# Down projection of an encoder layer: operands of products 5 and 6 split half by half, two stores on GpSimd's queue

## The chip, the cores and the metric

The kernel runs on one core of a Trainium2 chip. A core has a matrix engine (TensorE, in the profile PE, with its weight loads as PEld), a vector engine (VectorE, DVE), an engine for activation functions and scaled copies (ScalarE, ACT), a general engine (GpSimd, POOL) and an engine that here issues transfers (SyncE, SP). Each engine takes its instructions in a fixed order; semaphores make it wait for others. Transfers (DMA) are issued by an engine's queue and run beside the engines. On-chip memory is SBUF, with 128 partitions; matmuls accumulate in eight banks of PSUM.

The metric is the device time of one execution in microseconds (us): the median of the runs.

## The reference, cut to what matters

One hybrid encoder layer on 1024 positions of width 1024: a norm and an input projection, two groups of attention heads, an output projection and residual, then a gated MLP with a short convolution. The change lies at the end of the MLP, in the product with `w_down`:

```
def conv_ffn(h, w_up, conv_w, conv_b, w_down):
    u = h @ w_up
    u = lax.conv_general_dilated(u, conv_w[:, None, :], ..., feature_group_count=c) + conv_b
    gate, val = u[..., :D_FF], u[..., D_FF:]
    return (jax.nn.gelu(gate) * val) @ w_down

...
x = x + conv_ffn(rms_norm(x, norm2_g), w_up, conv_w, conv_b, w_down)
```

D_FF is 2816, so the last product is (1024 x 2816) by (2816 x 1024), in float32.

## The kernel before

**Seven products for eight.** Both MLP products are done as two-by-two blocks with seven block products in place of eight (a scheme with shared sums, its products numbered 1 to 7). The down projection runs them in the order 1, 5, 6, 3, 7, 2, 4. So product 1 comes first, and products 5 and 6 are the second and third. The contraction of 2816 is cut into 11 pairs of 128-row blocks, q = 0 to 10. One step is one product for one q: 7 x 11 = 77 steps, in the list `steps` (L1427), numbered m = 0 to 76 here. Steps 0 to 10 are product 1, steps 11 to 21 product 5, steps 22 to 32 product 6, steps 33 to 43 product 3, then 7, 2 and 4.

**float32 from two parts.** An operand is rounded to the matmul type (fp32r) by a copy on ACT, and what the rounding lost is taken by a subtraction on DVE. Three matmuls (high x high, high x low, low x high) then make one product. In `down` (L1474) a step makes 4 row tiles of 3 matmuls, 12 in all, each 128 x 128 by 128 x 512.

**What a step needs.** A block of `w_down` (128 x 512), a block of the gated activations from the scratch tensor `gscr` in DRAM (128 x 512, the stationary side of the matmuls), and for products 5 and 7 a second block of `w_down`, to be subtracted. The activations' sums and differences for the seven products were made earlier, on POOL, and stored to `gscr`; each product has its columns there (`place`, L1391).

**Loads.** `d_load` (L1432) issues two transfers of 256 KB, L1437 for `w_down` and L1438 for `gscr`, side by side into one of four load buffers `F_DR[m % 4]`. `d_load2` (L1440) issues the third, L1443, into one of three buffers `F_D2[q % 3]`. All are on SP's queue.

**Preparation.** `d_prep` (L1445) makes, where the product wants it, a difference on DVE (L1450): for product 5 into `F_T[q]`, which product 6 overwrites with its own and product 4 reads at the end. Then it splits both blocks in one go: the copy on ACT (L1460) and the subtraction on DVE (L1461), 1024 columns each, into one of six operand buffers `R_D[m % 6]`. For products 5 and 6 the first half of the source is `F_T[q]` and the second half lies in the load buffer, at `o + 512`; the two are given as one access pattern whose outer stride is the distance of the two places (L1459).

**Where things lie.** All of this is in two big arrays of SBUF, `bigf` (float32) and `bigr` (fp32r), at fixed columns. The columns of `bigf` that matter: `F_T[0..7]` at 4928 + 512 i; `F_T[8..10]` at 9024 + 512 i; `F_D2` at 3904, 4416 and 11072; `F_DR` at 14656, 15680, 16704 and 11584, 1024 columns each; the residual rows `C_11` at 12608 + 512 t, which are the same columns as two accumulators of the last pair of activations (called s1 and s3 in `gate_sums`).

**Order.** The program is written out step by step (L1594): matmuls of step m, preparation of step m + 3, subtrahend of step m + 6, loads of step m + 7, and what follows a product (`behind`, L1486): sums of finished banks with result rows on DVE (L1470), fetches of residual rows from `rscr` (L1467) in steps q = 5 to 8 of products 1, 5, 6 and 2, and result stores. A compiler pass derives the waits from which columns an instruction reads and writes, and fixes the order on each engine by its own estimate of when things are ready; so a queue's order is close to the program's, but not the same.

**The last pair of activations.** Its convolution, gate and sums come after the down projection has begun: `take(gate_sums(last), 4)` at m = 3 (L1604). `gate_sums` (L1393) stores the gated blocks (L1404, L1405), makes four sums of 128 x 512 on POOL (L1396, with two one-element instructions, L1401, that only order them) and stores two results of 1024 columns each, s1 at L1415 and s3 at L1419. All these stores are on SP's queue, ahead of the loads that follow in the program.

Of the kernel before, what the change touches and what calls it, by code (L numbers as in the profile page):

```python
# [14 lines left out]
AF = mybir.ActivationFunctionType  # L15
OP = mybir.AluOpType
# [7 lines left out]
NPAIR = NBLK  # L24
# [102 lines left out]
def tile_encoder_layer(ctx, tc, x, w_in, gains, outg, norm1_g, norm2_g, w_out, w_up, conv_w, conv_b,  # L127
# [14 lines left out]
    def emit(bounded):  # L142

        act = nc.scalar.activation
        vec = nc.vector
        gp = nc.gpsimd
        mm = nc.tensor.matmul
        dma = nc.sync.dma_start

        def f(off, n):  # L150
            return bigf[:, off:off + n]

        def r(off, n):
            return bigr[:, off:off + n]

        def rf(off, n):
            return bigr[:, off:off + n].bitcast(F32)

        def raw_ap(base, dims):
            return bass.AP(tensor=base.tensor, offset=base.offset,  # L160
                           ap=[list(base.ap[0])] + [list(d) for d in dims])

        def fp(off, *dims):
            return raw_ap(bigf[:, off:off + 1], dims)

        def rp(off, *dims):
            return raw_ap(bigr[:, off:off + 1], dims)

        def rfp(off, *dims):
            return raw_ap(bigr[:, off:off + 1].bitcast(F32), dims)  # L170
# [924 lines left out]
        for m in range(len(prods)):  # L1095
            c, n = prods[m]
# [159 lines left out]
        for gs in range(64 + lag + 1):  # L1256
# [15 lines left out]
            h1, s1 = divmod(gs - lag, 8)  # L1272
# [8 lines left out]
            h1, s1 = divmod(gs - lag - 1, 8)  # L1281
# [90 lines left out]
        def acc(j, u):  # L1372
            return F_ACC[(2 * j + u) % 6]
# [19 lines left out]
        def gate_sums(j):  # L1393
            e, o = acc(j, 0), acc(j, 1)
            s1, s3 = acc(j - 1, 0), acc(j - 1, 1)
            t = lambda d, a, b, op: gp.tensor_tensor(f(d, 512), f(a, 512), f(b, 512), op=op)  # L1396
            g = gscr[j // 2]

            def behind_sum(o):

                gp.tensor_tensor(f(o, 1), f(F_S[1], 1), f(F_S[1], 1), op=OP.add)  # L1401

            def halves():
                dma(g[:, 0:512], f(e, 512))  # L1404
                dma(g[:, 512:1536], f(o, 1024))  # L1405
                behind_sum(s1)
                t(s1, e + 512, o + 512, OP.add)

            def third():
                behind_sum(s3)  # L1410
                t(s3, e, e + 512, OP.subtract)

            def second():
                t(s1 + 512, s1, e, OP.subtract)
                dma(g[:, 1536:2560], f(s1, 1024))  # L1415

            def fourth():
                t(s3 + 512, o, s1 + 512, OP.subtract)
                dma(g[:, 2560:3584], f(s3, 1024))  # L1419

            return [halves, second, third, fourth]

# [22 lines left out]
        def d_prep(m):  # L1445
            if m >= len(steps):
                return
            n, q = steps[m]
            o, d, t = F_DR[m % 4], R_D[m % 6], F_T[q]
            sub = lambda out, i0, i1: vec.tensor_tensor(f(out, 512), f(i0, 512), f(i1, 512), op=OP.subtract)  # L1450
            if n == 5:
                sub(t, o, F_D2[q % 3])
            elif n == 6:
                sub(t, o, t)
            elif n == 7:
                sub(o, o, F_D2[q % 3])
            elif n == 4:
                sub(o, o, t)
            src = fp(t, [o + 512 - t, 2], [1, 512]) if n in (5, 6) else fp(o, [512, 2], [1, 512])  # L1459
            act(rp(d, [512, 2], [1, 512]), src, AF.Copy)  # L1460
            vec.tensor_tensor(rp(d + 1024, [512, 2], [1, 512]), src, rfp(d, [512, 2], [1, 512]), op=OP.subtract)  # L1461

        def o_rows(tt, hf):
            return perm_rows(out, tt, D)[:, 512 * hf:512 * hf + 512]
# [102 lines left out]
        for m in range(2, len(order)):  # L1567
            j, n = order[m]
            product(m)
            wu_prep(m + 4)  # L1570

            if n in (2, 4) or n == 3 and j % 2 == 0 or n == 1 and j % 2:
                take(dealt, 1)
            if n == 3 and j < NPAIR - 1:
                conv(j, 0)
                conv(j, 1)
                if j % 2:
                    gate(j, 0)
                    gate(j, 1)
                    dealt += gate_sums(j)  # L1580
            if j == NPAIR - 1:
                if n == 5:
                    for q in range(4):
                        d_load(q)
                if n == 4:
                    d_prep(0)
                    d_load(4)
                if n == 3:
                    d_prep(1)
                    d_prep(2)  # L1590
                    d_load(5)
                    d_load(6)
        last = NPAIR - 1
        for m in range(len(steps)):  # L1594
            n, q = steps[m]
            down(m)
            d_prep(m + 3)
            if m < 2:
                conv(last, m)
            if m == 2:  # L1600
                gate(last, 0)
                gate(last, 1)
            if m == 3:
                take(gate_sums(last), 4)  # L1604
            d_load2(m + 6)
            d_load(m + 7)
            behind(n, q)
# [68 lines left out]
```

## Time and profile before

| | us |
|---|---|
| median of 3 runs | 1301.46 |
| lowest, highest | 1300.12, 1302.01 |
| the profiled execution | 1300.51 |
| its span in the profile | 1298.7 |
| PE busy in the span | 1236.4 |
| DVE busy | 908.5 |
| ACT busy | 637.4 |
| POOL busy | 391.8 |
| first matmul of the down projection | 1047.74 |
| last matmul's end | 1286.76 |

The profile shows one execution. Times in its rows count from the span's start. A group row gives line, engine, operation, shapes and count, then the busy time in all and the mean of one instruction in ns, then the engine's idle time just before these instructions and what ended it. "bigf<-gscr" is a transfer from `gscr` into `bigf`. The rows "DMA to landing" give the time from the issue of a transfer to its completion. In a timeline row, what stands in brackets is the idle time before the instruction and what released it; x4 means that four were merged into one row.

### The profile page before, as it was taken

The page shows a single profiled execution, that of the slowest core. Times are in us where ns is not written, and L with a number is a line of the kernel's source. Part 1 is how long each engine was busy: PE and PEld are TensorE (multiplying, and loading weights), DVE is VectorE, ACT ScalarE, POOL GpSimd, SP SyncE. Part 2 cuts the span into 40 slices and gives each one's busy share as a digit, 9 for nine tenths or more (in the row PEclk, how much of TensorE's full clock was granted, in tenths as well). Part 3 has the DMA queues.
Part 4 walks back from the last instruction along what each step waited for, and adds up shares of the span by engine and source line. Part 5 has one row for each costly group of instructions (what it writes and reads, how often), then busy time and mean ns, then how long its engine had stood idle before and what let it go on. Part 6 is the DMA issues. An engine that isn't in the chain of part 4 may idle for free.

```text
span 1298.7 us, 18774 instructions
## 1 busy us (share of the span) xinstructions
PE 1236.4 (95%) x7063; PEld 1061.5 (82%) x7063; DVE 908.5 (70%) x1270; ACT 637.4 (49%) x1001; POOL 391.8 (30%) x300
## 2 busy tenths in 40 slices
PE   7999999999998889999999999999999998889996
PEld 7999998999997777888788888888888886657885
DVE  5988685124107779656999999999999964657672
ACT  7856554566556566535544453444443442234430
POOL 1610143000212230011465675665675530000000
PEclk9999999999999899999999999999999998999998
DMA  7126303000014444413222223232223357448970
GB/s 264 54 84 156 88 5 75 24 17 17 9 25 100 106 107 115 156 65 106 74 105 91 92 93 122 94 117 90 91 96 122 122 183 282 166 148 277 315 242 36
DMA packets 120935, 147.12 MB, mean 113 GB/s; under 512 B 51009, under 2 KB 79489, under 8 KB 120321
## 3 DMA queue, kind: packets, MB, share of 16 engines
q1 hardware_dynamic: 119617, 141.10, 33.6%
q0 software_dynamic: 1216, 4.72, 1.7%
q8 instruction: 57, 0.93, 0.3%
q14 instruction: 45, 0.37, 0.1%
HBM read 107.25 MB, written 33.82 MB: 109 GB/s over the span
## 4 chain that ended last, share of the span: by engine, by line
PE 55%; DVE 18%; issue 4%; DMA 4%; ACT 3%; POOL 1%; SPq 0%; ACTq 0%; DVEq 0%; POOLq 0%
PE ps L696 8%; PE ps L1349 6%; PE ps L1351 6%; PE ps L1350 6%; DVE bigf L1382 6%; PE ps L1481 4%; PE ps L1482 4%; PE ps L1480 4%; PE ps L701 3%; PE ps L702 2%; DVE bigf L1353 2%; PE ps L1004 2%; PE ps L1006 2%; PE ps L1005 2%; DVE bigr L1333 2%
## 5 line engine op out<-in xcount | busy, mean ns | idle before, releaser
L1349 PE MATMUL ps<-bigr 128*128 128x512 f32 x616 | 241.0, 391 | 6.5 <-DVE bigf L1353 5.9
L1350 PE MATMUL ps<-bigr 128*128 128x512 f32 x616 | 239.7, 389 | 0.0
L1351 PE MATMUL ps<-bigr 128*128 128x512 f32 x616 | 239.7, 389 | 0.0
L1382 DVE SCALAR_TENSOR_TENSOR bigf<-bigf 128x768 f32<-128x768 f32 (+1 forms) x176 | 178.8, 1074 | 26.5 <-ACT bigf L1380 26.4
L1332 ACT ACTIVATE bigr<-bigf 128x512 fp32r<-128x512 f32 x154 | 93.2, 625 | 139.3 <-POOL bigf L1324 70.4
L1460 ACT ACTIVATE bigr<-bigf 128x1024 fp32r<-128x1024 f32 x77 | 80.5, 1058 | 148.9 <-DMA bigf<-gscr 57.1
L1349 PEld LDWEIGHTS ps<-bigr 128*128 128x128 f32 x616 | 115.6, 188 | 35.1 <-DVE bigf L1353 9.3
L696 PEld LDWEIGHTS ps<-bigf 128*128 128x128 f32 x1024 | 131.9, 191 | 9.3 <-issue 0.3
L1351 PEld LDWEIGHTS ps<-bigr 128*128 128x128 f32 x616 | 115.6, 188 | 24.2
L1350 PEld LDWEIGHTS ps<-bigr 128*128 128x128 f32 x616 | 115.7, 188 | 23.5
L1461 DVE TENSOR_TENSOR bigr<-bigf,bigr 128x1024 fp32r<-128x1024 f32 x77 | 93.2, 1222 | 57.0 <-ACT bigr L1460 46.8
L1480 PE MATMUL ps<-bigr 128*128 128x512 f32 x308 | 114.1, 401 | 16.6 <-ACT bigr L1460 16.4
L696 PE MATMUL ps<-bigf 128*128 128x65 f32 x1024 | 129.1, 269 | 0.0
L421 PE MATMUL ps<-bigr 128*128 128x256 f32 x448 | 127.3, 284 | 1.2 <-ACT bigf L300 1.2
L1333 DVE TENSOR_TENSOR bigr<-bigf,bigr 128x512 fp32r<-128x512 f32 x112 | 125.3, 1136 | 3.2 <-ACT bigr L1332 2.5
L422 PE MATMUL ps<-bigr 128*128 128x256 f32 x448 | 126.9, 283 | 0.1
L423 PE MATMUL ps<-bigr 128*128 128x256 f32 x448 | 126.7, 283 | 0.0
L1481 PE MATMUL ps<-bigr 128*128 128x512 f32 x308 | 122.6, 400 | 1.4 <-DVE bigr L1461 0.9
L1482 PE MATMUL ps<-bigr 128*128 128x512 f32 x308 | 121.3, 395 | 0.0
L704 ACT ACTIVATE bigf<-ps 128x512 f32<-128x512 f32 x128 | 76.1, 597 | 78.9 <-PE ps L702 77.9
L421 PEld LDWEIGHTS ps<-bigr 128*128 128x128 f32 x448 | 85.8, 192 | 1.8 <-ACT bigf L300 1.6
L422 PEld LDWEIGHTS ps<-bigr 128*128 128x128 f32 x448 | 85.9, 192 | 0.3 <-DVE bigr L405 0.3
(215 smaller groups left out, 2441.8 us busy)
## 6 DMA issues: line engine op xcount, KB each, us to landing
bigf<-w_down SPq DMA_DIRECT2D x99, 256.0 KB, 3.7
bigf<-w_up SPq DMA_DIRECT2D x44, 512.0 KB, 3.6
bigf<-gscr SPq DMA_DIRECT2D x77, 256.0 KB, 3.7
gscr<-bigf SPq DMA_DIRECT2D x33, 512.0 KB, 2.6
bigf<-w_in SPq DMA_DIRECT2D x8, 1024.0 KB, 5.5
bigf<-x SPq DMA_DIRECT2D x15, 512.0 KB, 7.1
bigf<-w_out SPq DMA_DIRECT2D x8, 512.0 KB, 3.6
bigr<-bigr POOLq DMA_DIRECT2D x8, 512.0 KB, 4.7
```

Source lines behind the costliest of these rows:

```text
L421: mm(o, ah, wh, start=(k == 0 and t % 2 == 0 and n != 2), stop=False, skip_group_check=True)
L422: mm(o, ah, wl, start=False, stop=False, skip_group_check=True)
L423: mm(o, al, wh, start=False, stop=(k == 3), skip_group_check=True)
L696: mm(bank(ob, 65, 66 * i), f(slots[kt] + 128 * i, 128), f(F_VA + 132 * kt + 66 * kv, 65), start=(kt == 0 and i == 0), stop=(kt == 7), skip ...
L1333: (gp if n in (2, 4) and m > 3 else vec).tensor_tensor(rp(o + 512, [128, 4], [1, 128]), src, rfp(o, [128, 4], [1, 128]), op=OP.subtract)
L1349: mm(bank(b), wh, th, start=(k == 0 and n in (1, 5, 6, 7)), stop=False, skip_group_check=True)
L1350: mm(bank(b), wh, tl, start=False, stop=False, skip_group_check=True)
L1351: mm(bank(b), wl, th, start=False, stop=(k == 3), skip_group_check=True)
L1382: vec.scalar_tensor_tensor(f(a + o, n), f(i + d, n), w_, f(a + o, n), op0=OP.mult, op1=OP.add)
L1480: mm(o, ah, r(d, 512), start=(q == 0 and n in (1, 5, 2)), stop=False, skip_group_check=True)
L1481: mm(o, ah, r(d + 1024, 512), start=False, stop=False, skip_group_check=True)
L1482: mm(o, al, r(d, 512), start=False, stop=(q == NQ - 1), skip_group_check=True)
```

## The change

In `d_prep`, products 5 and 6 now split their two source blocks one after the other: two ACT copies and two DVE subtractions of 512 columns, each with a plain pattern, in place of one each of 1024 columns with the strided pattern. The other products keep one copy and one subtraction of 1024 columns, written without the two-level pattern; the columns are the same. In `gate_sums` the two stores of s1 and s3 of the last pair are issued by POOL's queue and no longer by SP's; for the other ten pairs nothing changes. Lines after L1397 move down by one.

```
@@ gate_sums @@
             g = gscr[j // 2]
+            put = gp.dma_start if j == NPAIR - 1 else dma
...
             def second():
                 t(s1 + 512, s1, e, OP.subtract)
-                dma(g[:, 1536:2560], f(s1, 1024))
+                put(g[:, 1536:2560], f(s1, 1024))
...
             def fourth():
                 t(s3 + 512, o, s1 + 512, OP.subtract)
-                dma(g[:, 2560:3584], f(s3, 1024))
+                put(g[:, 2560:3584], f(s3, 1024))
@@ d_prep @@
-            src = fp(t, [o + 512 - t, 2], [1, 512]) if n in (5, 6) else fp(o, [512, 2], [1, 512])
-            act(rp(d, [512, 2], [1, 512]), src, AF.Copy)
-            vec.tensor_tensor(rp(d + 1024, [512, 2], [1, 512]), src, rfp(d, [512, 2], [1, 512]), op=OP.subtract)
+            for i, src, w in ((0, t, 512), (512, o + 512, 512)) if n in (5, 6) else ((0, o, 1024),):
+                act(r(d + i, w), f(src, w), AF.Copy)
+                vec.tensor_tensor(r(d + 1024 + i, w), f(src, w), rf(d + i, w), op=OP.subtract)
```

## The prediction

> **What bounds the kernel now.** I read the page first, then stretches of the last stage, then the chain of waits there. The page gives the span of the profiled execution, a TensorE (PE) that is nearly always busy, and the slices in which it is not.
>
> ```profile
> span 1298.7 us, 18774 instructions
> ...
> PE   7999999999998889999999999999999998889996
> ...
> PEclk9999999999999899999999999999999998999998
> ```
>
> Slices of 32.5 us: the 34th to 36th digit of PE (1071 to 1169 us) are 8, and the granted clock dips in the first of them. That is in the down projection. Its 77 steps issue 12 matmuls each, 924 in all. I cut the stage at the start of its first matmul, after step 11, after step 37, and at its last matmul.
>
> ```profile
> core 0: us, PE busy (x) PEld busy (x) DVE busy (x) ACT busy (x) POOL busy (x), PEclk, DMA share, GB/s
> 1047.74:1080.38 32.64, 32.64 (x145) 26.84 (x143) 17.64 (x20) 8.50 (x8) 10.77 (x6) 1.00 0.65 228
> 1080.38:1180.67 100.29, 82.28 (x313) 59.91 (x313) 56.42 (x62) 31.46 (x31) 0.00 (x0) 0.93 0.58 194
> 1180.67:1286.77 106.10, 106.10 (x469) 87.65 (x467) 65.21 (x72) 36.66 (x35) 0.00 (x0) 1.00 0.67 226
> ```
>
> (x) counts matmuls that touch the stretch, so one at a border counts twice. The last stretch holds 39 steps, 468 matmuls in 106.10 us: 0.2267 us each, 2.72 us a step, with PE never idle. The first holds 12 steps at the same pace (32.64 / 12 = 2.72). The middle one holds steps 12 to 37, 312 matmuls, worth 312 x 0.2267 = 70.7 us at that pace; it took 100.29. So **29.6 us are lost there and nowhere else in the stage**: 18.0 us with PE idle (100.29 - 82.28), the rest as slow matmuls while the clock was at 0.93 or an operand was late. Steps 11 to 32 are products 5 and 6, the ones whose source pattern changes; steps 33 to 37, already plain, start with no lead and pay for the last of it.
>
> What does PE wait for? The first stall is that of step 12; then the chain of waits, in order of time:
>
> ```profile
> 1085.47 0.80 PE L1480 MATMUL ps<-bigr 128*128 128x512 f32 x1 [4.93 <-ACT bigr L1460]
> 1084.37 1.06 ACT L1460 ACTIVATE bigr<-bigf 128x1024 fp32r<-128x1024 f32 x1 [9.84 <-DMA bigf<-w_down]
> 1085.46 1.24 DVE bigr L1461
> ...
> 1086.71 0.33 SPq L1437
> ...
> 1087.09 2.93 DMA bigf<-gscr
> ...
> 1090.12 1.07 ACT bigr L1460
> ```
>
> The vector engine (DVE) ends a split (L1461) at 1086.70, the queue issues a load at 1086.71, its second half lands at 1090.02, and only then does the next copy on ScalarE (ACT, L1460) start. Which step is each? Steps load and copy in order, so a count up to that moment tells.
>
> ```profile
> L1438 SPq DMA_DIRECT2D bigf<-gscr x17: 327/424/740, 1003.9 to 1087.1; - x17
> L1460 ACT ACTIVATE bigr<-bigf x14: 1041/1059/1067, 1038.8 to 1090.1; 128x1024 fp32r<-128x1024 f32 x14
> ```
>
> The load of 1087.09 is the 17th, of step 16; the copy of 1090.12 is the 14th, of step 13. **The copy of step 13 waits for the data of step 16, which it does not use.** The pattern explains it: for products 5 and 6 the source is two pieces, t = F_T[q] and o + 512, written as one pattern with stride o + 512 - t. For step 13 (q = 2, buffer 1) the pieces lie at columns 5952 and 16192 of bigf; between them lies load buffer 0 (14656 to 15680), which step 16 fills. A dependence taken from the first to the last column of a pattern sees a conflict where none is. It binds both ways: the load of m + 4 waits for preparation m (truly: same buffer), preparation m + 1 waits for that load (falsely). A link is 0.4 us of queue, 2.9 of transfer, 1.07 of ACT and 1.24 of DVE, 5.7 us, against 2.72 us of matmuls. The spans include the earlier load buffer for buffers 0, 1 and 2, not for 3, so some three steps in four are bound; a late step is also fed in small pieces, as its L1481 waits for DVE.
>
> **Part 1, the split pattern (L1459 to L1461).** It removes the reach of the pattern, so step m waits for its own pieces only. It adds, in 22 steps, one ACT and one DVE instruction. The rows nearest to the new forms, and the old ones:
>
> ```profile
> L1460 ACT ACTIVATE bigr<-bigf 128x1024 fp32r<-128x1024 f32 x77 | 80.5, 1058 | 148.9 <-DMA bigf<-gscr 57.1
> L1332 ACT ACTIVATE bigr<-bigf 128x512 fp32r<-128x512 f32 x48 | 29.0, 625 | 46.7 <-POOL bigf L1324 27.1 <-PE ps L1350 19.3
> L1461 DVE TENSOR_TENSOR bigr<-bigf,bigr 128x1024 fp32r<-128x1024 f32 x77 | 93.2, 1222 | 57.0 <-ACT bigr L1460 46.8
> 1037.70 0.67 DVE L1333 TENSOR_TENSOR bigr<-bigf,bigr 128x512 fp32r<-128x512 f32 x1
> L1450 DVE TENSOR_TENSOR bigf<-bigf 128x512 f32<-128x512 f32 x44 | 29.9, 689 | 29.4 <-DMA bigf<-w_down 29.0
> ```
>
> ACT: 2 x 0.625 - 1.058 = +0.19 us a step; DVE: 2 x 0.67 - 1.22 = +0.12. That is 4.2 and 2.6 us of work in all, but the worst step needs 1.25 us of ACT and 0.69 + 1.34 + 0.69 = 2.7 us of DVE (difference, two halves, one sum into the result, the last in eight of the steps), under or at 2.72, so it hides behind the matmuls as long as preparation is ahead; if not, it costs 0.3 us for each step that PE waits for. The other five products keep the same 1024 columns, written plainly: nothing.
>
> Can loads keep up? Product 7 has the traffic of product 5 and is already plain:
>
> ```profile
> 1197.00:1226.90 29.90, 29.90 (x133) 24.77 (x132) 20.78 (x23) 11.58 (x11) 0.00 (x0) 1.00 0.91 317
> 1070.00:1080.00 10.00, 10.00 (x46) 8.29 (x45) 3.75 (x4) 2.12 (x2) 0.00 (x0) 1.00 0.98 343
> ```
>
> Its 11 steps ran at 2.72 us with three loads each (and four result stores). At 343 GB/s a 256 KB load takes 0.76 us: three make 2.3 us a step, four (the steps that also fetch rows of the residual) 3.06, 0.34 too much in four steps, 1.4 us that the lead covers. So in the steady state PE sets the pace. What is left is the entry, around step 12.
>
> **Part 2, the two stores on the queue of GpSimd (POOL), L1416 and L1420 after the change.** SyncE's queue (SP) now stands still behind them, since their sums are late:
>
> ```profile
> 1057.12 0.32 SPq L1405 DMA_DIRECT2D gscr<-bigf  x1
> 1064.47 0.32 SPq L1415 DMA_DIRECT2D gscr<-bigf  x1
> 1066.97 0.32 SPq L1419 DMA_DIRECT2D gscr<-bigf  x1
> 1067.39 0.38 SPq L1437 DMA_DIRECT2D bigf<-w_down  x1
> ...
> 1070.90 0.43 SPq L1467 DMA_DIRECT2D bigf<-rscr  x1
> 1071.43 0.38 SPq L1443 DMA_DIRECT2D bigf<-w_down  x1
> 1056.09 5.60 POOL L1401 TENSOR_TENSOR bigf<-bigf 128x1 f32<-128x1 f32 x1 [22.18 <-issue]
> 1063.15 3.79 POOL L1396 TENSOR_TENSOR bigf<-bigf 128x512 f32<-128x512 f32 x3
> 1057.01 4.62 DVE L1461 TENSOR_TENSOR bigr<-bigf,bigr 128x1024 fp32r<-128x1024 f32 x4
> ```
>
> From 1057.44 to 1067.39 it issues no load. Moved, the loads of steps 10, 11 and 12 go out when their buffers come free, with the DVE splits that end at 1058.2, 59.4 and 60.5: some 9 us earlier. But the residual rows of L1467 land where s1 lies, so they may not start until the store out of s1 has landed; on SP they, and all behind them, wait for POOL. Its price, from the rows of DMAs:
>
> ```profile
> 394.35 0.56 POOL L788 DMA_DIRECT2D bigr<-bigr  x1 [10.04 <-PE ps L892]
> bigr<-bigr POOLq DMA_DIRECT2D x8, 512.0 KB, 4.7
> gscr<-bigf SPq DMA_DIRECT2D x33, 512.0 KB, 2.6
> DMA to landing us min/median/max: 2.5/5.2/7.7
> ```
>
> From POOL a 512 KB transfer took 4.7 us, four small ones (last row, L344) 2.5 to 7.7; from SP 2.6. The second half of s1 is summed at 1064.4; 4.7 us later is 1069.1 (bounds 1066.9 and 1072.1), against 1070.90 for the rows now. So behind them part 2 gains 1.8 us, or loses 1.2, or gains 4.0. I take 1.8, by the transfer of the same size. POOL itself has nothing after these stores.
>
> **The entry, step by step.** PE is due at step 12 at 1080.38, and 2.72 us later at each one after. Step 12's last input is its subtrahend, now issued at 1071.43; with 1.8 us off and the 5.5 us its landing took, 1075.1; then 0.69 + 1.25 + 0.67 = 2.6 us: ready at 1077.7, in time. Loads for steps 13 to 15 follow at 0.76 us each (two or three a step, plus a row of the residual): ready by some 1080, 1083 and 1086 against 1083.1, 85.8 and 88.5. Step 16 loads into the buffer that step 12 leaves at 1077.7, behind four more residual rows (3.0 us) and 5.5 us of landing: 1086.2, subtrahend a little later, ready near 1090 against 1091.3. From there 2.3 us of loads meet 2.72 us of matmuls, and the lead grows. I leave 1 us for a step that just misses.
>
> ```profile
> DMA to landing us min/median/max: 5.5/5.5/5.5
> ```
>
> **Sum.** The profiled execution took 1300.51 us, 1.8 us around its span; 1300.51 - 29.6 + 1 = 1271.9. The median of the runs shown is 1301.46, 0.95 above: **1272.9 us**.
>
> **Rivals.** *A new wait behind POOL.* DVE and POOL get in each other's way: the L1401 row above, one element, took 5.60 us while DVE ran without a pause to 1061.63. With loads earlier, DVE splits steps 10 and 11 (1.2 + 2.0 us) just when POOL sums: POOL may be 3.2 us later, and the transfer 3.0 longer (7.7 for 4.7). The subtrahend of step 12 then lands at 1075.1 + 6.2 = 1081.3, and step 12 is ready at 1083.9, 3.5 us late; with a second step half as late 5. That is 1272 + 5 = 1277. [...]
>
> *Only part of the stall goes.* The compiler's order on each queue is fixed anew; a queue that waits in a worse order, or subtrahend buffers that come round every third step, could leave a third to a half of 29.6: 1282 to 1287. Against it: product 7, with the same buffers, shows no stall.
>
> *The waits are others' and stay* (the change doesn't do what it says). If the copy of step 13 still starts on the landing of step 16's load, the link of 5.7 us stays and grows by the added 0.19 + 0.12 us; three in four of 22 steps, 16 links, make 5 us: 1306.5, slower. It decides as soon as these links outlast 2.72 us, which they do at any length. Against it: from step 37 on, plain patterns with the same buffers never stall. A variant keeps the waits but hides the additions: 1301.
>
> **How the numbers follow.** Forecast 0.62, the wait behind POOL 0.19, part of the stall 0.10, slower 0.06, no change 0.03. Faster 0.91, the same 0.03 (within 0.2%, about what this kernel's measurement can tell from no change), slower 0.06. More than 29.6 us cannot come from this stall; with 1 us of scatter and no residue the low end is 1270. The high end takes in the rival behind POOL and the better half of the partial one: 1283. That holds 0.62 + 0.19 + 0.05, about 0.8 with some room for scatter.
>
> **What would show it.** Right: the stretch after step 11 at 46 matmuls in 10 us with the clock at 1.00, L1460 no longer idle behind a gscr load, 44 more instructions (22 on ACT, 22 on DVE), halves of 0.6 and 0.67 us; SP loading between 1057 and 1067. Wrong: a copy that starts on the landing of a load three steps on (the waits stay); L1467 late and PE idle near step 12 (POOL); a time above 1283.

## The result, and the profile after

| | before | after |
|---|---|---|
| median, us | 1300.79 (4 runs, 1299.90 to 1302.01) | 1268.59 (4 runs, 1267.77 to 1269.75) |
| ratio | | 0.9748, 95% interval 0.9734 to 0.9763 |
| the profiled execution, us | 1300.51 | 1268.52 |
| its span, us | 1298.7 | 1266.7 |
| first to last matmul of the down projection, us | 239.01 | 209.44 |
| end of the last matmul (its start plus 0.23 us, the pace of the stage) to end of span, us | 11.95 | 9.54 |

The kernel is 32.2 us faster. The forecast was 1272.9 with a range from 1270 to 1283; the result lies 4.3 us below the forecast and 1.4 us below the range. In the profiled executions, the first matmul of the stage starts at 1047.74 before and at 1047.75 after, so all of the gain comes later: 29.57 us inside the stage, 2.41 us behind its last matmul.

The page of after: the span, the busy time of each engine, and the 40 slices (now of 31.7 us).

```profile
span 1266.7 us, 18849 instructions
...
PE 1224.8 (97%) x7063; PEld 1060.7 (84%) x7063; DVE 911.0 (72%) x1292; ACT 640.8 (51%) x1023; POOL 393.8 (31%) x302
...
PE   7999999999999889999999999999999999999997
...
PEclk9999999999999999999999999999999999999999
```

The hole in PE's slices 34 to 36 is closed, and so is the dip of the granted clock there (0.93 over steps 12 to 37 before, 1.00 now). The count of instructions, which includes waits, is 75 above before's; the 44 that the change itself adds are counted below. The same cuts of the stage as before the change, at its first matmul, after step 11, after step 37 and at its last matmul (columns as in the prediction's table):

```profile
core 0: us, PE busy (x) PEld busy (x) DVE busy (x) ACT busy (x) POOL busy (x), PEclk, DMA share, GB/s
1047.75:1080.39 32.64, 32.64 (x146) 27.04 (x144) 24.51 (x29) 12.35 (x16) 12.78 (x8) 1.00 0.75 259
1080.39:1151.11 70.72, 70.72 (x314) 58.58 (x312) 54.13 (x78) 31.44 (x46) 0.00 (x0) 1.00 0.81 273
1151.11:1257.20 106.09, 106.09 (x469) 87.68 (x467) 63.06 (x70) 36.09 (x34) 0.00 (x0) 1.00 0.65 215
```

Read the second row against the prediction's: steps 12 to 37 took 100.29 us and now take 70.72, with PE busy for every one of them and the clock at 1.00. The rows above and below it have kept their lengths. That is the whole gain of the stage: 100.29 - 70.72 = 29.57. The stage now takes 209.44 us, 77 steps of 2.72, with PE never idle.

What the engines waited for in the stage, first before, then after (us in total, times, the longest):

```profile
ACT bigr L1460 <- DMA bigf<-gscr: 57.1, 17, 12.2
PEld ps L1480 <- ACT bigr L1460: 22.1, 14, 5.4
PE ps L1480 <- ACT bigr L1460: 16.4, 8, 4.9
```

```profile
ACT bigr L1461 <- PE ps L1483: 78.0, 47, 1.8
DVE bigf L1451 <- DMA bigf<-w_down: 26.2, 21, 4.1
...
ACT bigr L1461 <- DMA bigf<-gscr: 10.8, 8, 3.5
```

The direction has turned round. Before, the copy on ACT waited 57.1 us for loads, and PE waited for the copy. After, the copy waits for PE to release an operand buffer (78.0 us in 47 short waits), and PE is busy for the whole 209.44 us. No wait of PE on the copy is left in this list.

The groups of the split after, shapes apart:

```profile
L1461 ACT ACTIVATE bigr<-bigf 128x1024 fp32r<-128x1024 f32 x54 | 57.1, 1060 | 83.3 <-PE ps L1483 76.2 <-DMA bigf<-gscr 5.1 <-PE ps L1351 2.0
...
L1462 DVE TENSOR_TENSOR bigr<-bigf,bigr 128x512 fp32r<-128x512 f32 x44 | 29.8, 709 | 1.1 <-ACT bigr L1461 1.1
L1461 ACT ACTIVATE bigr<-bigf 128x512 fp32r<-128x512 f32 x44 | 25.7, 626 | 32.4 <-DVE bigf L1451 17.1 <-PE ps L1482 7.9 <-DMA bigf<-gscr 5.7
```

There are 44 halves on ACT and 44 on DVE where 22 whole instructions stood on each: the 44 more that were forecast. A half takes 626 ns on ACT and 709 on DVE (684 without the one that ran beside a sum on POOL and took 1777).

The two queues around the moved stores, first SP, then POOL, in order of time:

```profile
1057.12 0.32 SPq L1406 DMA_DIRECT2D gscr<-bigf  x1
1058.26 0.33 SPq L1438 DMA_DIRECT2D bigf<-w_down  x1
...
1061.81 0.42 SPq L1439 DMA_DIRECT2D bigf<-gscr  x1
1069.10 0.32 SPq L1468 DMA_DIRECT2D bigf<-rscr  x1
1069.52 0.38 SPq L1444 DMA_DIRECT2D bigf<-w_down  x1
```

```profile
1056.10 5.59 POOL L1402 TENSOR_TENSOR bigf<-bigf 128x1 f32<-128x1 f32 x1 [22.18 <-issue]
...
1063.16 3.00 POOL L1396 TENSOR_TENSOR bigf<-bigf 128x512 f32<-128x512 f32 x2
1066.11 0.58 POOL L1416 DMA_DIRECT2D gscr<-bigf  x1
1066.72 1.68 POOL L1396 TENSOR_TENSOR bigf<-bigf 128x512 f32<-128x512 f32 x1
1068.70 0.58 POOL L1420 DMA_DIRECT2D gscr<-bigf  x1 [0.30 <-POOL bigf L1396]
```

SP issues the loads of steps 10 to 12 between 1058.26 and 1061.81, where before they went out between 1067.39 and 1070.12. It then still stands until 1069.10, behind the residual rows that land in s1. DVE in that time (timeline of after):

```profile
1064.93 4.61 DVE L1462 TENSOR_TENSOR bigr<-bigf,bigr 128x1024 fp32r<-128x1024 f32 x3
1073.66 0.69 DVE L1451 TENSOR_TENSOR bigf<-bigf 128x512 f32<-128x512 f32 x1 [4.12 <-DMA bigf<-w_down]
```

DVE works to 1069.54 and then waits 4.12 us for the subtrahend of step 12, the load that went out behind the residual rows at 1069.52.

### The profile page after: what moved, and what is told of

Read it like the earlier page. It is cut to its first block, busy times and chain, and to the rows that moved or that the text cites. A ratio compares the mean times of both kernels' runs of the same rounds, so it can differ in the third digit from the quotient of the medians.

```text
span 1266.7 us, 18849 instructions
## 1 busy us (share of the span) xinstructions
PE 1224.8 (97%) x7063; PEld 1060.7 (84%) x7063; DVE 911.0 (72%) x1292; ACT 640.8 (51%) x1023; POOL 393.8 (31%) x302
## 4 chain that ended last, share of the span: by engine, by line
PE 61%; DVE 16%; issue 4%; ACT 2%; POOL 1%; DMA 0%; DVEq 0%; ACTq 0%; POOLq 0%
PE ps L696 9%; PE ps L1349 6%; PE ps L1351 6%; PE ps L1350 6%; DVE bigf L1382 6%; PE ps L1482 5%; PE ps L1481 5%; PE ps L1483 5%; PE ps L701 3%; PE ps L702 2%; DVE bigf L1353 2%; PE ps L1004 2%; PE ps L1006 2%; PE ps L1005 2%; DVE bigr L1333 2%
## 5 line engine op out<-in xcount | busy, mean ns | idle before, releaser
L1461 ACT ACTIVATE bigr<-bigf 128x1024 fp32r<-128x1024 f32 (+1 forms) x99 | 83.8, 867 | 115.8 <-PE ps L1483 78.0
L1462 DVE TENSOR_TENSOR bigr<-bigf,bigr 128x1024 fp32r<-128x1024 f32 (+1 forms) x99 | 97.4, 1004 | 24.1 <-ACT bigr L1461 22.4
```

## The experiments

All start from the changed kernel; e2 puts the old split back, and e7 adds to e4. Every ratio is to the kernel before, measured in the same round as the experiment. Line numbers are those of each kernel; around the split they differ by a few.

### One part at a time

**e1** keeps the split by halves and puts the two stores back on SP.

```
-            put = gp.dma_start if j == NPAIR - 1 else dma
+            put = dma
```

> The split patterns alone; all stores stay on SyncE's queue. Span theory (the reach of the two-piece pattern makes the whole loss): the stage from first to last matmul takes 209.4 to 211 us against 239.0 before, step 12 is ready about 1 us ahead, total 1269 to 1272.5 us; what is left to the changed kernel is its tail after the last matmul (9.5 us there, 11.9 before). Queue theory (the stores that block SyncE's queue start the loss): most of the 29.6 us stay, 1290 us or more. Halving theory (smaller pieces let the matrix engine start earlier): like the span theory.

**e2** keeps the stores on POOL and puts the strided split back.

```
-            for i, src, w in ((0, t, 512), (512, o + 512, 512)) if n in (5, 6) else ((0, o, 1024),):
-                act(r(d + i, w), f(src, w), AF.Copy)
...
+            src = fp(t, [o + 512 - t, 2], [1, 512]) if n in (5, 6) else fp(o, [512, 2], [1, 512])
+            act(rp(d, [512, 2], [1, 512]), src, AF.Copy)
...
```

> The two stores on GpSimd's queue alone; the two-piece pattern stays. Span theory: the copy of step 12 still waits for loads up to step 15, and each next one for a load three steps on; 25 to 30 us stay lost, total 1294 to 1302 us. Queue theory: the loss is gone, 1268 to 1275 us. Halving theory: 1294 to 1302 us.

Measured: e1 1270.75 us, ratio 0.9751 (0.9738 to 0.9764); e2 1299.45 us, ratio 0.9977 (0.9967 to 0.9987). The whole stage of e1, then e2's at the cuts of the first table (columns as above):

```profile
1049.64:1259.08 209.44, 209.44 (x925) 173.24 (x923) 139.41 (x176) 79.64 (x95) 10.77 (x6) 1.00 0.72 242
```

```profile
1081.00:1179.63 98.63, 82.85 (x314) 59.79 (x314) 56.50 (x62) 31.43 (x31) 0.00 (x0) 0.95 0.58 187
```

The split alone closes the whole hole: 209.44 us, PE never idle. The stores alone leave it: steps 12 to 37 still take 98.63 us in e2. So the first explanation one might have, that late loads behind the stores start the stall, falls. The chain of waits in e2 shows why; the loads of step 12 were issued by 1062.02 there, its subtrahend at 1070.13:

```profile
1076.79 4.91 DMA bigf<-w_down
...
1081.98 1.06 ACT bigr L1461
...
1084.33 0.33 SPq L1438
...
1084.70 2.90 DMA bigf<-gscr
...
1087.71 1.07 ACT bigr L1461
```

The copy of 1081.98 is step 12's. The chain puts its start down to the load issued at 1076.79, but the copy waits for several semaphores, and that load was complete only at 1082.26, after the copy had started. In the trace, the wait that ended last on ACT's queue ahead of this copy is the one for a residual row, issued at 1076.11, 6.0 us behind step 12's own last input, and landed at 1081.60; all others were met by then. The residual rows (`C_11`, from column 12608) lie between the two pieces of step 12 (5440 and 15168), so the copy waits for them without reading them. It was the same before the change: step 12's copy of 1084.37 started behind a residual row issued at 1078.56, which landed at 1084.11. Then the same links follow as before the change: a load issued at 1084.33, its partner landed at 1087.6, and the next copy at 1087.71.

How much reserve part 2 adds is seen in the lead of each step, the end of its last subtraction to the start of its first matmul, in us, worked out from the start and end of these instructions:

```
step      10     11     12     13     14     15     16     17
before   0.50   1.87  -1.21  -1.20  -1.21   0.21  -0.70  -1.21
after    7.71   8.12   4.23   5.75   4.75   4.37   4.08   4.40
e1       0.24   1.76   1.21   2.70   1.75   1.21   1.88   1.95
```

(A negative lead is a step whose first matmuls start on the copy, while DVE is still busy.) Without part 2, step 10 is ready only 0.24 us ahead of PE, step 12 1.21. That is enough, so part 2 buys no time in the stage.

### Halving, nearness or reach

The split by halves changes three things at once: the instruction is half as long, the dependence of a half is that of one place, and nothing reads both places any more. **e3** halves the instruction but lets each half read both places, 256 columns in each, so that its first and last columns lie as far apart as before.

```
+            for i in (0, 256) if n in (5, 6) else (0,):
+                w = 256 if n in (5, 6) else 512
+                src = fp(t + i, [o + 512 - t, 2], [1, 256]) if n in (5, 6) else fp(o, [512, 2], [1, 512])
+                act(rp(d + i, [512, 2], [1, w]), src, AF.Copy)
...
```

> The changed kernel, but each of the two halves takes 256 columns of both places by a two-piece pattern: as many and as large instructions as in the changed kernel (two copies, two subtractions of 512 columns), and the reach of before. Span theory: the waits are back and each link is longer by 0.2 to 0.3 us, 1294 to 1307 us. Halving theory: 1268 to 1273 us, as the changed kernel. Queue theory: 1268 to 1273 us.

**e4** doesn't halve at all: the difference is written over its block in the load buffer, so that both source blocks lie side by side, and one plain instruction of 1024 columns splits them. POOL copies the difference to `F_T[q]` for later products.

```
-                sub(t, o, F_D2[q % 3])
...
+            if n in (5, 7):
+                sub(o, o, F_D2[q % 3])
+            elif n in (4, 6):
+                sub(o, o, t)
+            if n in (5, 6):
+                gp.tensor_copy(f(t, 512), f(o, 512))
+            act(r(d, 1024), f(o, 1024), AF.Copy)
...
```

> The changed kernel, but not halved: products 5 and 6 write their difference over the load buffer's first half, GpSimd copies it to F_T for the later product, and one copy and one subtraction of 1024 plain columns split it. Span theory: no waits for later loads, stage at 209.4 to 211 us, 1268 to 1273 us. Halving theory: the loss of before is back, 1290 us or more. The added copy on GpSimd (about 1.3 us) runs beside ACT and DVE and costs nothing in either.

Measured: e3 1270.27 us, ratio 0.9756 (0.9740 to 0.9771); e4 1272.01 us, ratio 0.9768 (0.9753 to 0.9783). The stage of e3, and that of e4:

```profile
1046.22:1255.66 209.44, 209.44 (x925) 173.24 (x923) 141.99 (x176) 79.06 (x95) 11.93 (x8) 1.00 0.73 242
```

```profile
1047.81:1257.25 209.44, 209.44 (x925) 173.29 (x923) 142.34 (x154) 77.06 (x73) 36.05 (x30) 1.00 0.72 241
```

e4 has as few ACT and DVE instructions as before (73 and 154 against 95 and 176) and no stall: halving isn't what helps. e3 is the miss. By the prediction's own sentence, that a dependence is taken from the first to the last column, it should have kept the stall, at 1294 us or more. It has none. So that sentence, as it stands, is wrong: a pattern of two far pieces isn't always seen as all that lies between.

### Where the reach begins to count

What differs between the old pattern and e3's is the length of a piece, 512 columns against 256. **e5** and **e6** lie between the two and one column apart: two instructions again, each reading both places, of 297 and 215 columns in e5, of 296 and 216 in e6. In the compiled programs of these two, which carry for each instruction the semaphores that it waits for, the copies of 297 columns a piece wait for transfers of later steps, and those of 215, 216 and 296 do not; the runs put that to the chip.

```
+            i = 0
+            for w in (297, 215) if n in (5, 6) else (512,):
+                src = fp(t + i, [o + 512 - t, 2], [1, w]) if n in (5, 6) else fp(o, [512, 2], [1, 512])
+                act(rp(d + i, [512, 2], [1, w]), src, AF.Copy)
...
+                i += w
```

> The changed kernel, but the two instructions take 297 and 215 columns of both places by a two-piece pattern. In the compiled program the larger ones wait for transfers of later steps; the smaller do not. Waits theory (only waits for later steps' loads cost, whatever the pieces' size): the loss is back, stage 225 to 240 us, total 1284 to 1303 us. Halving theory (two instructions in place of one make the gain): 1267 to 1273 us.

> The same with 296 and 216 columns: one column is moved from the first instruction to the second in each place, reach and number of instructions as in the run with 297. In the compiled program no copy waits for a later step's load. Waits theory: stage 209.4 us, total 1267 to 1273 us. Reach theory (any two-piece pattern waits for all that lies between): 1284 to 1303 us. Halving theory: 1267 to 1273 us.

Measured: e5 1290.04 us, ratio 0.9900 (0.9885 to 0.9916); e6 1268.27 us, ratio 0.9736 (0.9721 to 0.9751). The stage of e5, then that of e6:

```profile
1049.67:1279.00 229.33, 214.55 (x925) 171.68 (x923) 142.21 (x176) 79.46 (x95) 12.79 (x8) 1.00 0.67 222
```

```profile
1045.95:1255.39 209.44, 209.44 (x925) 173.28 (x923) 141.90 (x176) 79.08 (x95) 11.94 (x8) 1.00 0.73 242
```

One column moved from one instruction to the other in 22 steps costs 21.8 us. The engines' work is the same within 0.4 us (DVE 142.21 against 141.90, ACT 79.46 against 79.08); what is new in e5 is that PE stands idle for 14.8 us and that the stage is 19.9 us longer. That is two thirds of the loss of before; why the rest doesn't come back stays open. Rows of ACT in e5's timeline, the copies of steps 12 and 13:

```profile
1076.53 0.56 ACT L1463 ACTIVATE bigr<-bigf 128x430 fp32r<-128x430 f32 x1 [8.29 <-DVE bigf L1451]
1082.98 0.70 ACT L1463 ACTIVATE bigr<-bigf 128x594 fp32r<-128x594 f32 x1 [5.88 <-DMA bigf<-w_down]
1085.33 0.56 ACT L1463 ACTIVATE bigr<-bigf 128x430 fp32r<-128x430 f32 x1 [1.65 <-DVE bigf L1451]
1088.20 0.70 ACT L1463 ACTIVATE bigr<-bigf 128x594 fp32r<-128x594 f32 x1 [2.31 <-DMA bigf<-gscr]
```

It is the copy of two times 297 columns that stands behind transfers; that of two times 215 goes through behind its DVE difference. The waits that ACT's queue makes ahead of these copies say the same (SP's transfers take eight semaphores in turn, in the trace of before numbers 99 to 102, 104 and 107 to 109, here DMAHW0 to 7; the traces hold these waits, and the compiled programs their names):

```
before, step 12:  ACTIVATE 128x1024   [waits DMAHW2,DMAHW3,DMAHW1,DMAHW4,DMAHW0,DMAHW5,DVE,DMAHW7,PE,Activation]
e5, step 12:      ACTIVATE 128x2x215  [waits DVE,DMAHW6,PE,Activation]
                  ACTIVATE 128x2x297  [waits DMAHW5,DMAHW3,DMAHW6,DMAHW2,DMAHW7,DMAHW1,DMAHW0]
e6, step 12:      ACTIVATE 128x2x296  [waits DVE,DMAHW7,PE,Activation]
                  ACTIVATE 128x2x216  [no wait of its own]
```

Before, the copy of step 12 waits for seven of the eight: DMAHW2 and 3 are the loads of step 15, and DMAHW1, 5, 0 and 4 four residual rows, none of which it reads; the last of these waits ended at 1084.13, 0.24 us before the copy started. In e6 it waits for one. So what sets e5 apart from e6 is the waits, and they stand in the program before it runs: seven for transfers ahead of step 12's copy of 297 columns a piece, one ahead of that of 296. What decides it, the length of a piece or another property that grows with it, was not shown, and neither was why the border lies there.

### What the tail is made of

The prediction had no term for the 2.41 us behind the last matmul. The rows that SP writes at the end of the program are small waits of the trace that the profile's views leave out. Counted from the end of the last matmul, in us:

```
         last result landed   SP's branch after it   end of span
before        5.46                  5.96                11.95
after         5.36                  5.43                 9.54
e1            5.52                  6.02                10.14
e2            5.51                  5.58                11.66
e4            5.43                  5.50                11.59
e7            5.22                  5.29                 9.40
e8            5.27                  5.85                10.16
```

Two things differ. Between landing and branch, before needs 0.50 us and after 0.07: SP checks the eight transfer semaphores in a fixed order, the same in the traces of before and after, about 0.07 us each, and the last result store fell on the second of them before, so that six checks come after it, and on the last of them after the change. Moving two stores to POOL shifts which transfer takes which semaphore. **e8** puts the store of s1 back on SP and leaves that of s3 on POOL, so that the last two results take the last and the first semaphore.

```
-                put(g[:, 1536:2560], f(s1, 1024))
+                dma(g[:, 1536:2560], f(s1, 1024))
```

> The changed kernel with one of the two stores back on SyncE's queue (that of s1). Stage 209.4 us. The last two result stores then fall on the last and the first of the eight semaphores that SyncE checks in a fixed order, so seven checks follow the first one's landing: tail 0.4 to 0.6 us over the changed kernel's 9.5, as with both stores on SyncE's queue (10.1), unless the code's second fetch comes in (then 11.9). Total 1268 to 1271.5 us.

Measured: 1270.04 us, ratio 0.9744 (0.9730 to 0.9759), stage 209.44, tail 10.16: landing to branch takes 0.58 as in e1 (0.50), where after takes 0.07. The order of the checks is worth 0.5 us.

From branch to the end, before, e2 and e4 need 6.0 to 6.1 us, all others 4.1 to 4.3. In those three, one of SP's closing waits comes some 1.9 us behind the one ahead of it; before, that is the step from 1295.36 to 1297.23, and an 8 KB transfer of instructions starts inside it, at 1295.75; the same holds in e2 (1294.36) and e4 (1265.79). SP executes 772 to 774 instructions in these three kernels, 775 to 787 in the others. The gap also moves with the count: it follows the fifth closing wait in e2 (772 instructions), the third before the change (773), the first in e4 (774). That speaks for a place in the code, at which, by the author's reading, SP waits for its next instructions. **e7** is e4 with eight more instructions on SP: the two loads of each of the first four steps of product 4 are issued in two pieces each, with the same bytes.

```
...
+            for i in (0, 256) if n == 4 and q < 4 else (0,):
+                c = 256 if n == 4 and q < 4 else 512
+                dma(f(o + i, c), w[:, i:i + c])
+                dma(f(o + 512 + i, c), g[:, i:i + c])
```

> The run with whole pieces near, whose tail after the last matmul was 11.6 us, with eight more instructions on SyncE's queue that move no more data: the loads of the first four steps of product 4 are cut in two. Code theory of the tail (1.85 us are lost where the place of the closing waits in SyncE's code makes a second fetch): the closing waits move in the code, the gap goes, tail 9.5 to 9.8 us, stage 209.4, total 2.0 us under the run with whole pieces near, 1268.5 to 1271 us. Work theory (the tail belongs to what the kernel does): tail 11.6 us, total as that run, 1270.5 to 1273 us.

Measured: 1269.60 us, ratio 0.9744 (0.9731 to 0.9758) against e4's 0.9768, stage 209.44, tail 9.40 against 11.59. With eight instructions more the tail is 2.2 us shorter in the profile, and the gap of 2.0 us among the closing waits is gone. This fits the place in the code; that SP waits for the transfer of instructions was not shown: after has one too, started at 1265.64, and there the closing waits go on 0.06 us apart.

## Where the prediction was right, and the step that failed

**Place and size of the stall: right.** 29.6 us were said to lie in steps 12 to 37; 29.57 came out of them, and nothing of it returned elsewhere in the stage.

**The false wait: right for this kernel, put too generally.** Copies did wait for later steps' loads (e2), and the waits went with the pattern (e1, e4). But "A dependence taken from the first to the last column of a pattern sees a conflict where none is" fails for e3 and e6, whose patterns reach as far. It holds for the 512-column pieces of the old code, and on the chip for 297; it doesn't for 296 or 256. The profile of before couldn't have told this, since all the two-piece sources of these copies had 512 columns. The prediction also named load buffers alone, while the copy of step 12, the first to stall, waited longest for a residual row.

**The cost of two instructions for one: right and hidden.** ACT 2 x 0.626 - 1.060 = +0.19 us a step, as forecast; DVE 2 x 0.709 - 1.241 = +0.18, where +0.12 was forecast from a single row; without the two splits that ran beside sums on POOL it is 2 x 0.684 - 1.221 = +0.15. No step waits for it.

**The entry: early enough, with more room than worked out.** Step 12 was ready at 1076.16 (forecast 1077.7), step 16 at 1087.19 (about 1090), each some 4 us ahead of PE. The residue of 1 us, for a step that just misses, wasn't needed; in e1, with part 2 undone, the least lead of step 12 and behind is still 1.21 us.

**Part 2: as forecast on the queue, nothing in the stage.** Steps 10 to 12 were loaded some 9 us earlier. The residual rows went out at 1069.10, the very time forecast, but by luck, through two errors that cancel. The store of s1 was issued at 1066.11 and not at 1064.4, and it landed in 2.93 us and not in 4.7. The sum that completes s1 ended at 1064.46 (before the change at 1064.45, and SP issued the store at 1064.47). But on POOL's own queue the store stands behind the next sum, the first of s3, which ran from 1064.42 to 1066.16. Without DVE beside it that sum takes 1.29 us, here 1.74: so some 1.2 us of the delay come from the order of POOL's queue, for which the prediction had no term, and 0.45 from the slowing. By time alone, after and e1 can't be told apart (0.9748 and 0.9751); from the stage's first matmul on, the profiles differ by 0.6 us, all of it tail.

**The wait behind POOL: a real slowing that met nothing.** Two sums of POOL took 1.74 and 1.68 us beside DVE, against 1.29 without it, and the one-element instruction 5.59, and the DVE split beside the first of these sums took 2.31 us where the others took 1.22; so the two engines do get in each other's way. The transfer of 7.7 us that this rival reckoned with did not come: the first store landed 2.93 us after its issue, against 2.6 from SP, with DVE at work all the time, and the second 4.01 us after its issue, with DVE idle for most of it.

**The step that failed is the sum, and with it the bound.** "More than 29.6 us cannot come from this stall; with 1 us of scatter and no residue the low end is 1270" was true of the stall, and was used as if nothing outside the stage could move. The sum kept what lies behind the last matmul at its old length; that stretch shrank by 2.41 us, of which the order of checks and a little earlier landing make 0.5, and the gap among SP's closing waits 1.9. Neither is what the change was made for: the gap went with SP's instruction count, 773 before and 783 after. The rest of the 4.3 us: 1.0 for the residue that wasn't needed, and 0.9 because 0.95 was added for a median above the profiled execution, while after the median lies 0.07 above it. With the tail left open by 2 us on either side, the range would have held the result.

## What to carry to other kernels

Where a copy waits for a load of data it doesn't read, look at its access pattern: two far pieces in one instruction can be taken by the compiler for everything between, as here with 512 and 297 columns a piece, and two plain instructions, 0.2 us dearer here, or pieces placed side by side, free it. Read the waits from the compiled program, since neither the reach of a pattern nor the number of instructions alone tells whether they are there. Don't trust the transfer that a chain names where a copy waits for several: look which wait ended last. When a change adds or moves instructions or transfers on a queue, leave some 2 us for the end of the program, as here, which can shift though nothing in it was touched.

## What the runs showed of the hardware that was not expected

- **The end of the program went with the number of instructions on SP.** With 772 to 774 of them its closing waits hold a gap of 1.9 to 2.0 us, with 775 to 787 none (three kernels and seven). Eight added transfers, of no more data, shortened a kernel's tail from 11.59 to 9.40 us.
- **Which semaphore the last result takes is worth 0.5 us,** as SP checks eight in a fixed order at about 0.07 us each: from landing to branch 0.50 us before, 0.07 after.
- **POOL's two stores were not as slow as its earlier transfers.** 512 KB from SBUF to DRAM landed in 2.93 and 4.01 us from POOL and in 2.6 from SP, where 512 KB inside SBUF had taken 4.7 from POOL, in 64 rows of 8 KB and not in 128 of 4 KB. Sums on POOL took 1.29 us with DVE idle and 1.68 to 1.74 beside it.
